# The low-part and the high-part products of split weights, in runs of eight blocks

## The chip, the cores and the metric

The kernel runs on one core of a Trainium2 chip. The metric is the time of one execution on the device, in microseconds. It is the median of three executions, and it is set beside one more execution that the hardware profiler recorded.

## The reference

The reference is a decoder trunk of two layers over one sequence of 256 tokens with 1024 channels, in float32. Cut to what matters here:

```
for i in (0, 1):
    hn = rmsnorm(h, norm_mix[i])
    mixed = short_conv_mixer(hn, ...) if i == 0 else dilated_attention_mixer(hn, ...)
    h = h + mixed
    h = h + square(relu(rmsnorm(h, norm_mlp[i]) @ mlp_w_up[i])) @ mlp_w_down[i]
    h = h + sigmoid(rmsnorm(h, norm_ple[i]) @ ple_w_gate[i]) * (p[i] @ ple_w_proj[i])
return rmsnorm(h, norm_final)
```

The short convolution needs three products of the width of h and one more; the attention has three groups of eight heads (a window of 128 with step 1, of 512 with step 4, of 2048 with step 16), so its query, key and value weights are 1024 x 9216. The MLP's weights are 1024 x 4096 and 4096 x 1024. Nearly all of the work is matrix products of weights by 256 columns of activations.

## The kernel before

**Products in two parts.** Every float32 weight and every activation is split in two: a high part rounded to the matmul's format (`whi`, made by ScalarE, L332) and the rest (`wlo`, made by VectorE, L333, through the helper `sub` at L281). A product is the sum of three matmuls: low weights by high activations, high weights by low activations, high weights by high activations. The weights come from memory in slabs of eight 128 x 128 blocks, in the order in which the plan first needs them; `split_to` splits them up to five slabs ahead of their use.

**The plan.** `make_plan` writes out one list of steps by hand. A step is a block (one 128 x 128 block of weights, by 256 columns of activations) or a `("do", ...)` step, which reads finished sums and makes the next activations. All engines work through instructions issued in this order; a scheduler may move those of the other engines, but the matmuls keep it.

**Kinds of blocks.** There are three:
- `"n"`: three matmuls of 256 columns, into one half of a PSUM bank.
- `"w"`: two matmuls. The activations' high and low parts lie next to each other (`x[2]`, 512 columns), so the high weights take both in one matmul of 512 columns, and the low weights take the high part in one of 256 columns. They go into a bank of their own, whose two halves `sums` adds later. There are 1296 of these blocks by the plan: 512 for the products `acc_u` of the two layers' MLP up, 384 for `acc_d` (down, all but the last quarter of each), 336 for `acc_qk` (queries and keys of heads 1 to 7) and 64 for `acc_X` (one third of the convolution's input product).
- `"t"`: the activations are the stationary operand and the weights move, 384 or 512 columns, three matmuls (`acc_v`, and `acc_g` and `acc_p` of the last stage).

The `"w"` blocks come in pairs, half 0 and half 1 (two neighbouring blocks of weights, the same activations). Half 0 is issued low then high, half 1 high then low, so that on TensorE two low products (256 columns each) and two high products (512 columns each) alternate.

Of the kernel before, what the change touches and what calls it, by code (L numbers as in the profile page):

```python
# [31 lines left out]
HURRY = 250  # L32
URGENT = ("gate_out", "mix_out", "down_out", "begin")
LOOK = 5
RAW_BUFS, SPLIT_BUFS, ACT_BUFS, PAIR_BUFS = 5, 6, 13, 20


# [168 lines left out]
def width(key):  # L206
    return {"v": GROUPS, "gate1": 4, "proj1": 4}.get(key, 1)
# [32 lines left out]
def tile_trunk(ctx: ExitStack, tc: tile.TileContext, plan, slabs, ap, out):  # L240
# [25 lines left out]
    def bank(name):  # L266
        return psum.tile([P, 2, S], F32, tag="ps", name=name)
# [9 lines left out]
    def flat(t):  # L277
        return t.rearrange("p i s -> p (i s)")
# [15 lines left out]
    acc, left, opened = {}, {}, set()  # L294
    for op in plan:
        if op[0] != "do":
            key = ((*op[4], op[5]), 0) if op[0] == "w" else (op[4], op[5] if op[0] == "n" else 0)
# [7 lines left out]
    offsets, n = [], 0  # L305
# [19 lines left out]
    def split_to(last):  # L325
        while len(parts) <= min(last, len(slabs) - 1):
            si = len(parts)
            load_to(si + RAW_BUFS - 1)
            t, width = loaded[si]
            hi = split_pool.tile([P, SLAB * P], F32R, tag="whi", name=f"whi{si}")  # L330
            lo = split_pool.tile([P, SLAB * P], F32R, tag="wlo", name=f"wlo{si}")
            nc.scalar.activation(hi[:, :width], t[:, :width], AF.Copy)  # L332
            sub(lo[:, :width], t[:, :width], hi[:, :width])  # L333
            parts.append((hi, lo))

    def weights(item):
        si, at = place[item]
        split_to(si + min(LOOK, 1 + si // 3))
        hi, lo = parts[si]
        n = width(item[0]) * P  # L340
        return hi[:, at : at + n], lo[:, at : at + n]

    def block(kind, key, k, col, name, half, operand, m=0, cuts=1):
        name = (*name, half) if kind == "w" else name
        if name not in opened:
            acc[name] = bank("acc_" + "_".join(map(str, name)))
        left[name, half if kind == "n" else 0] -= 1
        whi, wlo = weights((key, k, col))
        x = state[operand][k // 2]
        if kind == "n":  # L350
            dst = acc[name][:, half, :]
            products = ((dst, wlo, x[0][:, k % 2, :]), (dst, whi, x[1][:, k % 2, :]), (dst, whi, x[0][:, k % 2, :]))
        elif kind == "w":

            dst = acc[name]
            products = ((dst[:, 0, :], wlo, x[0][:, k % 2, :]), (flat(dst), whi, flat(x[2][:, k % 2, :, :])))

            products = products[::-1] if half else products
        else:
            n = width(key) * P // cuts  # L360
            whi, wlo = (t[:, m * n : (m + 1) * n] for t in (whi, wlo))
            dst = flat(acc[name])[:, :n]
            xhi, xlo = (t[:, k % 2, half * P : (half + 1) * P] for t in x[:2])
            products = ((dst, xhi, whi), (dst, xhi, wlo), (dst, xlo, whi))
        for n, (to, a, b) in enumerate(products):
            nc.tensor.matmul(  # L366
                to,
                a,
                b,
                start=n == 0 and name not in opened,  # L370
                stop=n == len(products) - 1 and left[name, half if kind == "n" else 0] == 0,
                skip_group_check=True,
            )
            opened.add(name)
# [391 lines left out]
        scores=scores, turn=turn, spread=spread, values=values,  # L766
        last_load=last_load, turn_h=turn_h, last_gate=last_gate, last_out=last_out, last_rms=last_rms, last_scale=last_scale,
    )
    for op in plan:
        if op[0] != "do":  # L770
            block(*op)
        elif op[1] in URGENT:
            with tc.high_priority(offset=HURRY):
                steps[op[1]](*op[2:])
        else:
            steps[op[1]](*op[2:])
# [87 lines left out]
```

## Time and profile before

| What | Value |
|---|---|
| median of three executions | 795.62 us (795.31 to 795.94) |
| the profiled execution, its own time | 797.34 us |
| its span, from the first to the last instruction | 795.5 us |
| TensorE (PE) busy | 776.2 us, 98% of the span |
| weight loads of TensorE (PEld) | 711.6 us, 89% |
| VectorE (DVE), ScalarE (ACT), GpSimd (POOL) busy | 582.1, 436.6, 177.2 us |
| mean granted clock of TensorE | 0.994 of full speed |

The profile tells for each instruction when it started and how long it took, and for each wait what ended it. A matmul's end is modelled and matmuls overlap, so a matmul's cost is read from the distance between the starts of neighbours, not from its own duration. The profiled execution's span and its own time are 1.8 us apart, and that time is 1.7 us above the median.

### The profile page before, as it was taken

What the parts mean: (1) busy time and instruction counts of PE and PEld (TensorE: products, weight loads), DVE (VectorE), ACT (ScalarE), POOL (GpSimd) and SP (SyncE); (2) the same over time, 40 slices, a digit from 0 to 9 for tenths busy, and PEclk for the clock granted to TensorE, in tenths of its full rate; (3) what the DMA queues carried; (4) which work ended last, traced back from release to release, by engine and by line L of the source; (5) the groups of instructions that cost most, each with busy time, mean ns of one, the idle gap of its engine ahead of it and who ended that gap; (6) DMA issues with size and microseconds to landing.
All of it is one profiled execution on the core that took longest, in us unless ns stands there. A gap on an engine that the chain in (4) does not pass through costs nothing.

```text
span 795.5 us, 12797 instructions
## 1 busy us (share of the span) xinstructions
PE 776.2 (98%) x4986; PEld 711.6 (89%) x4986; DVE 582.1 (73%) x818; ACT 436.6 (55%) x672; POOL 177.2 (22%) x117
## 2 busy tenths in 40 slices
PE   8999999999999999996999999999999999999996
PEld 7999998888888999986999999999988888888985
DVE  6987789898556669747678679679598887555555
ACT  7654565565444447527647546646475555444453
POOL 0000000000000000298587677678000000000001
PEclk9999999999999999998999999999999999999999
DMA  8866555656556555643464455456556655555521
GB/s 277 287 211 193 183 187 181 198 187 196 185 186 188 185 163 168 203 128 115 150 186 144 154 180 159 159 159 200 174 159 189 198 188 191 185 185 189 184 78 54
DMA packets 41676, 140.98 MB, mean 177 GB/s; under 512 B 4752, under 2 KB 5136, under 8 KB 41616
## 3 DMA queue, kind: packets, MB, share of 16 engines
q1 hardware_dynamic: 41616, 140.17, 55.7%
q8 instruction: 39, 0.64, 0.3%
q14 instruction: 21, 0.17, 0.1%
HBM read 139.10 MB, written 1.05 MB: 176 GB/s over the span
## 4 chain that ended last, share of the span: by engine, by line
PE 87%; DVE 5%; POOL 3%; ACT 2%; issue 2%; DMA 1%; SPq 0%; POOLq 0%; DVEq 0%; ACTq 0%
PE acc_d L366 23%; PE acc_u L366 22%; PE acc_qk L366 13%; PE acc_v L366 7%; PE acc_o L366 6%; PE acc_g L366 5%; PE acc_B L366 2%; PE acc_X L366 2%; DVE wlo L281 2%; PE acc_C L366 2%; POOL rot L612 2%; PE tp L662 1%; PE o L683 1%; PE sc L644 1%; ACT whi L332 1%
## 5 line engine op out<-in xcount | busy, mean ns | idle before, releaser
L281 DVE TENSOR_TENSOR wlo<-raw,whi 128x1024 fp32r<-128x1024 f32 (+3 forms) x273 | 364.5, 1343 | 130.0 <-ACT whi L332 127.9
L332 ACT ACTIVATE whi<-raw 128x1024 fp32r<-128x1024 f32 (+3 forms) x273 | 276.3, 1018 | 201.4 <-PE acc_d L366 82.0
L366 PE MATMUL acc_d<-u,whi 128*128 128x512 f32 (+1 forms) x640 | 166.8, 351 | 0.0
L366 PE MATMUL acc_u<-x,whi 128*128 128x512 f32 x512 | 161.0, 396 | 0.0
L366 PE MATMUL acc_qk<-x,whi 128*128 128x512 f32 (+1 forms) x432 | 122.9, 371 | 0.0
L438 POOL TENSOR_TENSOR n<-v,power 128x4 f32<-128x4 f32 (+1 forms) x6 | 6.5, 1085 | 512.2 <-DVE v L458 509.4
L366 PEld LDWEIGHTS acc_u<-x,wlo 128*128 128x128 f32 x512 | 96.4, 188 | 22.4
L366 PEld LDWEIGHTS acc_d<-u,wlo 128*128 128x128 f32 x512 | 96.9, 189 | 17.0
L366 PE MATMUL acc_d<-u,wlo 128*128 128x256 f32 x512 | 111.8, 279 | 0.0
L366 PE MATMUL acc_u<-x,wlo 128*128 128x256 f32 x512 | 101.3, 278 | 0.0
L366 PEld LDWEIGHTS acc_d<-u,whi 128*128 128x128 f32 x640 | 98.5, 190 | 0.0
L612 POOL TENSOR_TENSOR rot<-qk,sinr 16x512 f32<-16x512 f32 x48 | 87.0, 1813 | 3.3
L366 PEld LDWEIGHTS acc_qk<-x,wlo 128*128 128x128 f32 x384 | 72.4, 188 | 14.2
L366 PE MATMUL acc_qk<-x,wlo 128*128 128x256 f32 x384 | 82.5, 281 | 0.0
L366 PEld LDWEIGHTS acc_u<-x,whi 128*128 128x128 f32 x512 | 78.0, 189 | 0.1
L366 PE MATMUL acc_v<-whi,x 128*128 128x384 f32 x256 | 69.8, 343 | 0.0
L366 PEld LDWEIGHTS acc_qk<-x,whi 128*128 128x128 f32 x432 | 66.1, 189 | 0.0
L609 POOL TENSOR_TENSOR qk<-qk,cosr 128x512 f32<-128x512 f32 x24 | 37.9, 1578 | 57.9 <-DVE qk L386 44.6
L366 PEld LDWEIGHTS acc_v<-whi,x 128*128 128x128 f32 x256 | 47.4, 191 | 0.0
L366 PE MATMUL acc_o<-y,whi 128*128 128x256 f32 x256 | 46.0, 284 | 0.0
L366 PE MATMUL acc_v<-wlo,x 128*128 128x384 f32 x128 | 43.3, 339 | 0.0
L618 POOL TENSOR_TENSOR qk<-qk,rot 48x512 f32<-48x512 f32 x24 | 42.8, 1784 | 1.7
(164 smaller groups left out, 1029.6 us busy)
## 6 DMA issues: line engine op xcount, KB each, us to landing
raw<-in_w SPq DMA_DIRECT2D x232, 512.0 KB, 3.7
raw<-in_w SPq DMA_DIRECT2D x32, 384.0 KB, 3.1
raw<-in_w SPq DMA_DIRECT2D x7, 256.0 KB, 5.7
h<-in_xT SPq DMA_DIRECT2D x4, 256.0 KB, 6.0
out<-ht SPq DMA_DIRECT2D x4, 256.0 KB, 2.0
pt<-in_pT SPq DMA_DIRECT2D x2, 256.0 KB, 4.6
mask<-in_mask SPq DMA_DIRECT2D x2, 256.0 KB, 4.3
gain<-in_gain SPq DMA_DIRECT2D x2, 256.0 KB, 4.2
```

The source lines that it names most:

```text
L281: nc.vector.tensor_tensor(out, a, f32(b), ALU.subtract)
L332: nc.scalar.activation(hi[:, :width], t[:, :width], AF.Copy)
L366: nc.tensor.matmul(to, a, b, start=n == 0 and name not in opened, stop=n == len(products) - 1 and left[name, half if kind == "n" else 0] == 0,
L438: nc.gpsimd.tensor_tensor(y, v, power[:, : v.shape[1]], ALU.pow)
L609: nc.gpsimd.tensor_tensor(t, p, both(cosr), ALU.mult)
L612: nc.gpsimd.tensor_tensor(r[dst : dst + 16], p[src : src + 16], sinr[src : src + 16].unsqueeze(1).to_broadcast([16, 2, S]), ALU.mult,)
L618: nc.gpsimd.tensor_tensor(t[:48], t[:48], r[:48], ALU.add)
L644: nc.tensor.matmul(ps[:, (g + 1) * P : (g + 2) * P], t[:, 0, own], t[:, 1, own], start=True, stop=True)
L662: nc.tensor.transpose(ps[n // 2][:, n % 2, b * P : (b + 1) * P], sm[:, n * P : (n + 1) * P], ident)
L683: nc.tensor.matmul(ps[:, 0, b * P : (b + 1) * P], v12[:, b, g * P : (g + 1) * P], t[:, g, b * P : (b + 1) * P], start=False, stop=g == 1, ...
```

## The change

The new function `blocks` takes a run of `"w"` blocks and issues first all their low products, then all their high ones. The loop over the plan collects `"w"` blocks until eight are together or the next step is not one. The other kinds are issued as before. The number, the shapes and the operands of the matmuls stay the same; what changes is their order, which matmul opens and which ends the sum of a bank, and with it when a bank is ready to be read.

```
+RUN = 8
...
+    def blocks(ops):
+
+        for part in (0, 1):
+            for op in ops:
+                block(*op, part=part)
+
-    def block(kind, key, k, col, name, half, operand, m=0, cuts=1):
+    def block(kind, key, k, col, name, half, operand, m=0, cuts=1, part=None):
...
-        left[name, half if kind == "n" else 0] -= 1
+        left[name, half if kind == "n" else 0] -= part != 0
...
-            products = ((dst[:, 0, :], wlo, x[0][:, k % 2, :]), (flat(dst), whi, flat(x[2][:, k % 2, :, :])))
-
-            products = products[::-1] if half else products
+            products = ((dst[:, 0, :], wlo, x[0][:, k % 2, :]), (flat(dst), whi, flat(x[2][:, k % 2, :, :])))[part:][:1]
...
-                stop=n == len(products) - 1 and left[name, half if kind == "n" else 0] == 0,
+                stop=part != 0 and n == len(products) - 1 and left[name, half if kind == "n" else 0] == 0,
...
-    for op in plan:
-        if op[0] != "do":
+    run = []
+    for op, behind in zip(plan, [*plan[1:], ("do",)]):
+        if op[0] == "w":
+            run.append(op)
+            if behind[0] != "w" or len(run) == RUN:
+                blocks(run)
+                run = []
+        elif op[0] != "do":
             block(*op)
```

How the instructions stand now is seen at two places. The first is TensorE in the MLP up of layer 0, third pair of column blocks (`acc_u_2_0` and `acc_u_2_1` are the banks of half 0 and half 1, `x1_0` and `x1_1` two pairs of activation tiles, `whi43` and `wlo43` the parts of one slab). Before, eight matmuls in a row:

```order
L366 MATMUL acc_u_2_0_1494<-x1_0_1205,wlo43_1343 128x256
L366 MATMUL acc_u_2_0_1494<-x1_0_1205,whi43_1342 128x512
L366 MATMUL acc_u_2_1_1503<-x1_0_1205,whi43_1342 128x512
L366 MATMUL acc_u_2_1_1503<-x1_0_1205,wlo43_1343 128x256
L366 MATMUL acc_u_2_0_1494<-x1_0_1205,wlo43_1343 128x256
L366 MATMUL acc_u_2_0_1494<-x1_0_1205,whi43_1342 128x512
L366 MATMUL acc_u_2_1_1503<-x1_0_1205,whi43_1342 128x512
L366 MATMUL acc_u_2_1_1503<-x1_0_1205,wlo43_1343 128x256
```

And now, in the same place, the last four low products of a run and its first four high ones:

```order
L371 MATMUL acc_u_2_0_1494<-x1_1_1227,wlo43_1343 128x256
L371 MATMUL acc_u_2_1_1502<-x1_1_1227,wlo43_1343 128x256
L371 MATMUL acc_u_2_0_1494<-x1_1_1227,wlo43_1343 128x256
L371 MATMUL acc_u_2_1_1502<-x1_1_1227,wlo43_1343 128x256
L371 MATMUL acc_u_2_0_1494<-x1_0_1205,whi43_1342 128x512
L371 MATMUL acc_u_2_1_1502<-x1_0_1205,whi43_1342 128x512
L371 MATMUL acc_u_2_0_1494<-x1_0_1205,whi43_1342 128x512
L371 MATMUL acc_u_2_1_1502<-x1_0_1205,whi43_1342 128x512
```

Equal widths now follow each other eight at a time, and neighbouring matmuls always write to different banks. A run of eight here uses one slab, as its eight blocks did before.

The second place is VectorE where the softmax of head 0 is made (`sm0_0`, `sm0_1` the scores of the two halves of the tokens, `st...` their row statistics, `qk_1_2` the sums of head 1's third group, `wlo132` a slab to be split). Before:

```order
L386 TENSOR_TENSOR qk_1_2_3964<-acc_qk_1_2_0_3888,qk_1_2_3964 128x256
L647 ISA sm0_0_3940,st0_0_0_3941<-sc0_0_3934,mask0_3461 128x512
L647 ISA st0_0_0_3941 128x1
L386 TENSOR_TENSOR qk_1_2_3964<-acc_qk_1_2_1_3897,qk_1_2_3964 128x256
L650 TENSOR_SCALAR st1_0_0_3942<-st0_0_0_3941 128x1
L647 ISA sm0_1_3955,st0_0_1_3956<-sc0_1_3949,mask1_3463 128x512
L647 ISA st0_0_1_3956 128x1
L281 TENSOR_TENSOR wlo132_3977<-raw132_3834,whi132_3976 128x1024
L650 TENSOR_SCALAR st1_0_1_3957<-st0_0_1_3956 128x1
```

And now:

```order
L391 TENSOR_TENSOR qk_1_2_3964<-acc_qk_1_2_0_3888,qk_1_2_3964 128x256
L391 TENSOR_TENSOR qk_1_2_3964<-acc_qk_1_2_1_3896,qk_1_2_3964 128x256
L652 ISA sm0_0_3940,st0_0_0_3941<-sc0_0_3934,mask0_3461 128x512
L652 ISA st0_0_0_3941 128x1
L282 TENSOR_TENSOR wlo132_3977<-raw132_3834,whi132_3976 128x1024
L655 TENSOR_SCALAR st1_0_0_3942<-st0_0_0_3941 128x1
L652 ISA sm0_1_3955,st0_0_1_3956<-sc0_1_3949,mask1_3463 128x512
L652 ISA st0_0_1_3956 128x1
L655 TENSOR_SCALAR st1_0_1_3957<-st0_0_1_3956 128x1
```

The second sum of `qk_1_2` and the split of slab 132 moved ahead; the nine instructions up to the second negated maximum (the last row) are the same ones.

## Rows read from the trace of the kernel before

**Rows 1.** The page, busy us of each engine, share of the span, instructions.
```profile
PE 776.2 (98%) x4986; PEld 711.6 (89%) x4986; DVE 582.1 (73%) x818; ACT 436.6 (55%) x672; POOL 177.2 (22%) x117
```

**Rows 2.** Waits of TensorE, first two of five: us in total, times, longest.
```profile
PE tp L662 <- ACT sm L653: 7.0, 1, 7.0
PE acc_p L366 <- DVE wlo L281: 2.2, 3, 1.4
```

**Rows 3.** Chain that ended last: start us, us, what, number of matmuls.
```profile
38.62 5.58 PE acc_X L366 x32
...
84.14 23.04 PE acc_o L366 x192
...
129.71 66.89 PE acc_u L366 x384
196.60 89.92 PE acc_d L366 x576
...
394.75 6.24 PE acc_v L366 x36
...
777.33 2.04 PE acc_g L366 x9
```

**Rows 4.** A stretch of MLP up: busy us of each engine, granted clock.
```profile
core 0: us, PE busy (x) PEld busy (x) DVE busy (x) ACT busy (x) POOL busy (x), PEclk, DMA share, GB/s
129.71:196.60 66.89, 66.89 (x386) 58.44 (x386) 58.72 (x89) 40.06 (x64) 0.00 (x0) 1.00 0.61 189
```

**Rows 5.** Order of time, PE, MLP up: start us, us, instructions merged.
```profile
139.90 0.39 PE L366 MATMUL acc_u<-x,wlo 128*128 128x256 f32 x2
140.13 0.63 PE L366 MATMUL acc_u<-x,whi 128*128 128x512 f32 x2
140.59 0.40 PE L366 MATMUL acc_u<-x,wlo 128*128 128x256 f32 x2
```

**Rows 6.** Order of time, PE, where 512 columns follow a run of 256.
```profile
757.86 0.40 PE L366 MATMUL acc_g<-whi,x 128*128 128x512 f32 x1
...
759.02 0.62 PE L366 MATMUL acc_g<-whi,x 128*128 128x512 f32 x2
...
760.15 0.39 PE L366 MATMUL acc_g<-wlo,x 128*128 128x512 f32 x1
```

**Rows 7.** Order of time, PE, 512 columns a little behind transposes.
```profile
764.00 0.40 PE L366 MATMUL acc_g<-wlo,x 128*128 128x512 f32 x1
...
766.31 0.39 PE L366 MATMUL acc_g<-whi,x 128*128 128x512 f32 x1
```

**Rows 8.** Order of time, PE, where 256 columns follow a run of 512.
```profile
785.78 0.39 PE L366 MATMUL acc_g<-whi,x 128*128 128x512 f32 x1
786.01 0.28 PE L366 MATMUL acc_p<-whi,p 128*128 128x256 f32 x1
786.12 0.28 PE L366 MATMUL acc_p<-wlo,p 128*128 128x256 f32 x1
786.24 0.40 PE L366 MATMUL acc_p<-whi,p 128*128 128x256 f32 x2
786.48 0.28 PE L366 MATMUL acc_p<-wlo,p 128*128 128x256 f32 x1
```

**Rows 9.** Weight loads of two groups: busy us, mean ns of one, idle before.
```profile
L366 PEld LDWEIGHTS acc_u<-x,wlo 128*128 128x128 f32 x512 | 96.4, 188 | 22.4
L366 PEld LDWEIGHTS acc_u<-x,whi 128*128 128x128 f32 x512 | 78.0, 189 | 0.1
```

**Rows 10.** Order of time, VectorE, before the stall at head 0.
```profile
363.93 0.68 DVE L647 CUSTOM_DVE_ANT_0 sm<-sc,mask 128x512 f32<-128x512 f32 x1
...
364.53 0.42 DVE L386 TENSOR_TENSOR qk<-acc_qk,qk 128x256 f32<-128x256 f32 x1
...
365.53 1.69 DVE L281 TENSOR_TENSOR wlo<-raw,whi 128x1024 fp32r<-128x1024 f32 x1
367.15 0.14 DVE L650 TENSOR_SCALAR st<-st 128x1 f32<-128x1 f32 x1
```

**Rows 11.** Order of time, ScalarE, the last exponential before the stall ends.
```profile
367.33 0.72 ACT L651 ACTIVATE sm<-sm,st 128x512 f32<-128x512 f32 x1 [1.29 <-DVE st L650]
```

## The prediction

> **What bounds the kernel now.** I read the page's busy times first: TensorE is busy for 98% of the span [rows 1]. The second view is TensorE's waits: the longest is one stall of 7.0 us before the transposes of head 0, and the next, 2.2 us, lies at the start [rows 2]. So the time is a queue of matmuls on one engine, and an edit that keeps their number counts only by what it does to the distance between the starts of neighbours. The third view is the chain of waits in order of time, because its long pieces give that distance as a mean over hundreds [rows 3]. The reader is to see four numbers there:
> - 256 columns behind 256 columns: 23.04 us / 192 = 120.0 ns each (`acc_o`).
> - One `"w"` block in today's order: 66.89 us / 192 blocks = 348.4 ns (`acc_u`, 384 matmuls); `acc_X` gives 5.58 / 16 = 348.8. `acc_d` is the sum of both: 192 blocks at 348.4 ns and 192 matmuls at 120 ns make 89.9 us, and 89.92 stand there.
> - 384 columns behind 384: 6.24 / 36 = 173.3 ns (`acc_v`).
> - 512 columns behind 512: 2.04 / 9 = 226.7 ns (`acc_g`).
>
> From 256 to 384 and from 384 to 512 columns each step adds 53.3 ns, so in a stretch of one width a matmul costs 13.3 ns plus its columns at 0.417 ns. By that, a block would cost 120.0 + 226.7 = 346.7 ns, and it costs 348.4. The fourth view, TensorE's instructions in order of time, shows how: two low products take 0.23 us from start to start and two high ones 0.46 us [rows 5], that is 115 and 232 ns each. In the mixture the 512s cost some 6 ns more than in a stretch of their own, and the 256s some 5 ns less. The difference of the sums, 1.7 ns a block, is what the order costs today.
>
> **The change part by part.** Nothing is added or removed: the 1296 `"w"` blocks keep their two matmuls. By the order of the changed program they stand in 161 runs of eight and two of four, as much as 162 runs of eight, and every run uses one slab. So there are 162 places where 512s follow 256s, and not 648.
>
> *Eight low products.* In a stretch of their own they cost 8 x 120.0 = 960 ns. The first ones behind 512s are cheaper: at the end of the program four matmuls of 256 columns behind 512s take 786.48 - 786.01 = 0.47 us [rows 8], where four at 120 take 0.48. So 10 ns are given back, as the two low products give back today (0.23 for 0.24). I take 950 ns.
>
> *Eight high products.* In steady state 8 x 226.7 = 1813 ns. No row shows more than two 512s of this kind in a row; the nearest are the 512s of the last stage, where the activations are stationary and the weights move. There the first 512s behind 256s are dear: the five from 757.86 to 759.02 take 232 ns each, the five from there to 760.15 take 226 [rows 6]. That is 5 x 232 - 5 x 226.7 = 27 ns for the transition, after which the steady cost is reached. In the stretch from 764.00 to 766.31 ten of them take 2.31 us [rows 7], 44 ns over ten steady ones, so 35 ns for eight. At the other end, if only the first two paid, as many as stand together today (0.46 us for 0.453), it would be some 10 ns. I take 27 ns, because that stretch follows 256-column matmuls as the runs will.
>
> *The run.* 950 + 1813 + 27 = 2790 ns, against 8 x 348.4 = 2787 ns today: +3 ns a run, or 162 x 3 = **+0.5 us**. With 10 ns for the transition it is 2773, -14 a run, -2.3 us; with 35 it is 2798, +11 a run, +1.8 us. The main case is thus no change within about 2 us: the few transitions that remain cost more each, because more 512s stand behind them to pay.
>
> *When things are needed.* A run begins with its low products, as a pair did, so `wlo` of a slab is needed at the same moment; `whi` is needed 8 x 120 = 0.96 us later instead of 0.12. No split is due earlier, and raw tiles and split buffers turn over with the slab as before. In MLP up TensorE is busy for the whole 66.89 us while VectorE has 8 us and ScalarE 27 us free [rows 4]; that cover hides the splits, and without it each slab would show up to VectorE's split, 1.69 us [rows 10]. Where an MLP begins, the low parts of the activations are needed 0.84 us later. No wait of this kind is in [rows 2], so I count nothing.
>
> *When sums are ready.* Half 0's last product now ends one 512 before half 1's, 0.23 us, and not 0.35. Its two reading steps start 0.12 us later, on engines for which TensorE does not wait in these stages. The banks opened for half 1 are taken 0.12 us earlier; nothing in [rows 2] waits for a bank. I count nothing.
>
> *The stall at head 0.* TensorE waits there for ScalarE's scaled exponentials, which follow the second exponential at 367.33 [rows 11], and that follows VectorE's second negated maximum at 367.15 [rows 10]. VectorE's order ahead of it changes: the sum (0.42 us) and the split (1.69 us) each move ahead of a score step (0.68 us), but the same instructions stand before the negated maximum. So it comes at the same time; the first exponential comes later and can push the second by at most its own overlap, some 0.3 us. I take 0 and keep 0.3 for the range.
>
> The sum is +0.5 us. It is made against the profiled execution's span of 795.5 us (797.34 as its own time, 1.7 above the median). Applied to the median of the runs shown, 795.62, it gives 796.1 us.
>
> **The rivals.**
> - *The 512s stay at 233 ns, the 256s go to 120: slower.* The place is inside the run of high products. Here the price of a 512 would hang on what it is (weights stationary, both activation parts moving) and not on its neighbours; two of them together cost 0.46 us today [rows 5]. The low products lose the cheap position behind 512s. A run is then 8 x (120 + 232.5) = 2820 ns, +33 ns, +5.3 us, 800.9 us. It decides if the fourth to eighth 512 of a run still cost over 230 ns. Against it: 256s cost 120 whether weights or activations move in them [rows 3, 8], and the 13.3 ns hold at three widths, so the moving operand does not set the price. Chance 0.15.
>
>   [...]
> - *Only transitions cost: faster.* If the 1.7 ns a block were the price of today's 648 transitions and a longer run paid no more at each, 162 of them would keep a quarter, and 3/4 x 1.7 x 1296 = 1.7 us are saved: 793.9 us. For it: the 512s do settle at 226.7. Against it: [rows 6] and [rows 7] show five to ten dear ones at a transition, not two. Chance 0.28.
> - *Both the cheap rates hold: much faster.* Low products at 115 and high at 226.7 would give 162 x 8 x (348.4 - 341.7) = 8.7 us, 786.9 us. Against it: every long stretch of 256s runs at 120. Chance 0.04.
> - *A wait elsewhere appears*, from the new order on VectorE and ScalarE: about 1 to 3 us slower. Chance 0.05.
>
> **How the numbers follow.** The main case has 0.48, by itself from 794.4 to 797.7: a transition of 17 ns makes a run 2780 ns, -7 ns, -1.2 us; one of 35 ns gives +1.8 us, and the stall 0.3 more. Cheaper transitions are the second rival. A measurement of this kernel can tell about 0.2%, 1.6 us, from no change. Of the main case 0.08 lies above that and 0.40 within. Of the second rival, whose time lies on the bound of 794.0, 0.17 lies below and 0.11 within. The first rival and three fifths of the last are slower; the third is faster. Faster: 0.17 + 0.04 = 0.21; slower: 0.08 + 0.15 + 0.03 = 0.26; within: 0.40 + 0.11 + 0.02 = 0.53. The range goes from 793.5, where a transition costs 10 ns or a little more, to 800.9, the first rival.
>
> **What would show it.** In order of time, in MLP up: low products of a run start 115 to 120 ns apart and mostly 120; the first four or five high ones 230 to 236, the last ones 226 to 227; the chain's piece of 384 matmuls takes 66.8 to 67.1 us. If all eight high ones stay at 232, the first rival is right, and the piece takes 67.7 us. If the high ones fall to 227 from the third on, it takes 66.5. The stall at head 0 stays at 7 us. What would make the prediction wrong besides is a cost that today's order never shows, such as a dearer switch from the low to the high products of one slab.

## The result and the profile after

The changed kernel takes 798.3 us (median of eight runs, 797.68 to 799.01), the kernel before 795.95 us (median of eight, 795.19 to 796.28). The ratio is 1.0029 [1.002, 1.0038], so the change costs 2.3 us (1.6 to 3.0). The forecast was 796.1 us, with a range from 793.5 to 800.9; the time lies inside the range, but above the 0.2% within which the main case was to lie. The differences in us here and below are those of the ratio, with its interval; they can lie up to 0.7 us from the difference of the two medians.

The profiled execution of the changed kernel has a span of 795.9 us and 797.68 us as its own time, the lowest of the eight; the profiled one of before has 795.5 and 797.34, above all eight of before. So the two spans, 0.4 us apart, say little, and the pieces have to be compared one by one. One piece that differs and has nothing to do with the change is the start: this piece of `acc_X` starts at 36.85 us, where it started at 38.62 [rows 3]. The waits for the first split weights, 2.2 us before, are missing in this trace. The second experiment below has the order of before up to there, and its piece starts at 36.85 us too.

The first view is the page's busy times of the kernel after, us, share of the span and instructions:

```profile
PE 777.0 (98%) x4986; PEld 715.6 (90%) x4986; DVE 583.0 (73%) x818; ACT 439.0 (55%) x672; POOL 179.1 (23%) x117
```

TensorE is busy for 0.8 us more than in [rows 1], with the same 4986 matmuls. The second view is TensorE's waits of the kernel after (us in total, times, longest):

```profile
PE tp L667 <- ACT sm L658: 8.7, 1, 8.7
PE warm L510 <- DVE power L506: 1.0, 1, 1.0
```

The stall at head 0 was to stay at 7.0 us [rows 2] and takes 8.7. The wait of 2.2 us at the start is gone; that is the start told of above. The third view is the chain of the kernel after (start us, us, what, number of matmuls):

```profile
36.85 5.59 PE acc_X L371 x32
...
82.41 23.04 PE acc_o L371 x192
...
128.05 67.04 PE acc_u L371 x384
195.09 90.07 PE acc_d L371 x576
...
601.25 67.05 PE acc_u L371 x384
```

The piece of MLP up takes 67.04 and 67.05 us in the two layers, against 66.89 [rows 3]: 349.2 ns a block, not 348.4. The granted clock is 1.00 in it, as it was [rows 4]. `acc_o`, which holds no blocks of the changed kind, has not moved. The fourth view is TensorE's instructions in order of time in that piece:

```profile
140.02 2.00 PE L371 MATMUL acc_u<-x,whi 128*128 128x512 f32 x8
141.86 1.11 PE L371 MATMUL acc_u<-x,wlo 128*128 128x256 f32 x8
142.81 2.00 PE L371 MATMUL acc_u<-x,whi 128*128 128x512 f32 x8
144.65 1.12 PE L371 MATMUL acc_u<-x,wlo 128*128 128x256 f32 x8
```

From start to start, eight high products take 1.84 us (140.02 to 141.86) and eight low ones 0.95 (141.86 to 142.81). Averaged by their place in the run, over the 135 runs of eight that follow a 512 and are followed by a 256, the distance from each start to the next is, in ns:

```
place in the run      1      2      3      4      5      6      7      8     sum
low products        113.4  119.2  120.0  120.0  120.0  120.0  120.0  120.0   952.5
high products       233.3  235.9  228.3  232.5  230.8  226.7  226.7  226.8  1841.0
```

A run is 2793.5 ns, the forecast was 2790, and before it was 2787. So the mechanism is the forecast one: five dear 512s, then the steady 226.7. The size is 6.3 ns a run instead of 3, and 162 x 6.3 = 1.0 us instead of 0.5.

The fifth view is VectorE in order of time before the stall ends, in the kernel after (start us, us, instruction and how many are merged in the row; what it waited for in brackets):

```profile
358.89 0.70 DVE L282 TENSOR_TENSOR qk<-qk,qk 128x512 fp32r<-128x512 f32 x1 [8.48 <-ACT qk L410]
359.50 0.75 DVE L391 TENSOR_TENSOR qk<-acc_qk,qk 128x256 f32<-128x256 f32 x2
360.18 3.17 DVE L282 TENSOR_TENSOR wlo<-raw,whi 128x768 fp32r<-128x768 f32 x2
363.27 0.74 DVE L391 TENSOR_TENSOR qk<-acc_qk,qk 128x256 f32<-128x256 f32 x2
363.93 0.67 DVE L652 CUSTOM_DVE_ANT_0 sm<-sc,mask 128x512 f32<-128x512 f32 x1
...
364.54 2.32 DVE L282 TENSOR_TENSOR wlo<-raw,whi 128x1024 fp32r<-128x1024 f32 x1
...
366.85 0.68 DVE L652 CUSTOM_DVE_ANT_0 sm<-sc,mask 128x512 f32<-128x512 f32 x1
...
367.56 0.15 DVE L655 TENSOR_SCALAR st<-st 128x1 f32<-128x1 f32 x1
```

The same stretch of before, of which [rows 10] showed the end:

```profile
360.23 0.69 DVE L281 TENSOR_TENSOR qk<-qk,qk 128x512 fp32r<-128x512 f32 x1 [8.47 <-ACT qk L405]
360.84 0.42 DVE L386 TENSOR_TENSOR qk<-acc_qk,qk 128x256 f32<-128x256 f32 x1
361.23 0.96 DVE L281 TENSOR_TENSOR wlo<-raw,whi 128x768 fp32r<-128x768 f32 x1
362.11 0.42 DVE L386 TENSOR_TENSOR qk<-acc_qk,qk 128x256 f32<-128x256 f32 x1
362.45 1.23 DVE L281 TENSOR_TENSOR wlo<-raw,whi 128x1024 fp32r<-128x1024 f32 x1
```

From the split of head 1's first group to the second negated maximum it was 360.23 to 367.15, 6.92 us [rows 10]; now it is 358.89 to 367.56, 8.67 us: 1.75 us more, as much as the stall grew. The instructions are the same, and two of them are longer. The splits of the two slabs behind the first sums took 0.96 and 1.23 us, and now 0.96 and 2.23, merged into 3.17 above; the split behind the first score step took 1.69 and now 2.32. Together that is 5.49 us (3.17 + 2.32) where it was 3.88, 1.61 more. In MLP up, where GpSimd is idle [rows 4], all 24 splits of 128x1024 in the trace of before took 1.21 to 1.23 us.

What lies beside them is on GpSimd. Its rows in order of time, before:

```profile
362.67 2.13 POOL L609 TENSOR_TENSOR qk<-qk,cosr 128x512 f32<-128x512 f32 x1 [3.14 <-DVE qk L386]
364.88 3.47 POOL L612 TENSOR_TENSOR rot<-qk,sinr 16x512 f32<-16x512 f32 x2
```

And after:

```profile
360.33 1.93 POOL L614 TENSOR_TENSOR qk<-qk,cosr 128x512 f32<-128x512 f32 x1 [2.13 <-DVE qk L391]
362.34 3.44 POOL L617 TENSOR_TENSOR rot<-qk,sinr 16x512 f32<-16x512 f32 x2
365.85 2.13 POOL L623 TENSOR_TENSOR qk<-qk,rot 48x512 f32<-48x512 f32 x1
367.95 1.26 POOL L614 TENSOR_TENSOR qk<-qk,cosr 128x512 f32<-128x512 f32 x1
```

GpSimd's rotary step of head 1's second group (a product with the cosine, two with the sine, an addition) waits for both sums of `qk_1_1`. With the products in runs the second sum follows the first at once, ahead of the split of 768 columns, where it stood behind it. So the rotary step starts 1.4 us after the split of `qk` (360.33 - 358.89), and not 2.4 us (362.67 - 360.23).

The rows fit a strict taking of turns between a split and a product on GpSimd, whole instructions at a time, the one that begins first going at its own speed. GpSimd's product with the cosine takes 1.26 us where no split stands beside it, as at 367.95 in the kernel after. VectorE's sums, with one operand in PSUM, took no longer beside a product: the two at 363.27 in the kernel after take 0.74 us together inside a product with the sine, and the two at 359.50, beside none, 0.75. Follow the ends:

- Before, the split of 1024 columns at 362.45 is first and takes 1.23 us, to 363.68; the product that begins at 362.67 ends at 364.80, 1.12 us behind that. Only the split at 365.53 [rows 10] comes second, in the middle of the first product with the sine (364.88 to 366.14), and takes 1.69.
- After, the split at 360.18 is first, the product with the cosine ends at 362.26 behind it, and the second split ends at 363.35, 1.1 us behind the product: it came second. The third split begins at 364.54, and ends at 366.86, 1.1 us behind the end of the products with the sine at 365.78: second again, by nearly a whole product. GpSimd's addition, which begins at 365.85, ends 1.1 us behind the split, at 367.98.

So two splits wait out most of a product each, where one waited for part of one: the split that began first took 1.23 us, those that began second 2.23 and 2.32. The turns are the author's reading of these rows; why the two engines hold each other up is not shown.

This stall also has a price behind it. TensorE's granted clock is 0.50 from 366.18 to 373.00 us before and from 365.66 to 372.49 after, and 1.00 ahead of that and behind. It fell while TensorE was idle in the stall (from 361.84 us before and from 360.51 after) and rose while it worked again. The transposes that end the stall start at 368.81 and 369.23, so 4.2 us of work ran at the low clock before and 3.3 after. That gave 0.42 us back to this trace of the kernel after: the blocks behind start at 373.78 in both. In the second experiment below the low clock lasts until 374.25, over 5.5 us of work. So the same stall does not cost the same in each trace.

### The profile page after: what moved, and what is told of

The parts are those of the page before. It is cut to its first block, busy times and chain, and to the rows that moved or that the text cites. A ratio compares the mean times of both kernels' runs of the same rounds, so it can differ in the third digit from the quotient of the medians.

```text
span 795.9 us, 12768 instructions
## 1 busy us (share of the span) xinstructions
PE 777.0 (98%) x4986; PEld 715.6 (90%) x4986; DVE 583.0 (73%) x818; ACT 439.0 (55%) x672; POOL 179.1 (23%) x117
## 4 chain that ended last, share of the span: by engine, by line
PE 89%; POOL 3%; DVE 3%; ACT 2%; issue 1%; DMA 0%; SPq 0%; POOLq 0%; DVEq 0%; ACTq 0%
PE acc_d L371 23%; PE acc_u L371 22%; PE acc_qk L371 13%; PE acc_v L371 7%; PE acc_o L371 6%; PE acc_g L371 5%; PE acc_B L371 3%; PE acc_X L371 3%; PE acc_C L371 3%; POOL rot L617 2%; DVE wlo L282 1%; PE tp L667 1%; PE o L688 1%; PE sc L649 1%; POOL qk L623 1%
## 5 line engine op out<-in xcount | busy, mean ns | idle before, releaser
L371 PE MATMUL acc_d<-u,whi 128*128 128x512 f32 (+1 forms) x640 | 142.2, 349 | 0.0
L371 PE MATMUL acc_u<-x,whi 128*128 128x512 f32 x512 | 128.2, 392 | 0.0
L371 PEld LDWEIGHTS acc_u<-x,whi 128*128 128x128 f32 x512 | 92.1, 189 | 16.5
L371 PE MATMUL acc_qk<-x,whi 128*128 128x512 f32 (+1 forms) x432 | 101.5, 368 | 0.0
L371 PE MATMUL acc_d<-u,wlo 128*128 128x256 f32 x512 | 89.8, 282 | 0.0
L371 PEld LDWEIGHTS acc_d<-u,wlo 128*128 128x128 f32 x512 | 76.9, 191 | 3.8
L371 PEld LDWEIGHTS acc_u<-x,wlo 128*128 128x128 f32 x512 | 69.6, 190 | 4.7
L371 PE MATMUL acc_u<-x,wlo 128*128 128x256 f32 x512 | 71.4, 282 | 0.0
L371 PE MATMUL acc_qk<-x,wlo 128*128 128x256 f32 x384 | 61.0, 284 | 0.0
L371 PEld LDWEIGHTS acc_qk<-x,wlo 128*128 128x128 f32 x384 | 54.3, 190 | 2.3
```

The lines of the kernel that those rows point to most:

```text
L371: nc.tensor.matmul(to, a, b, start=n == 0 and name not in opened, stop=part != 0 and n == len(products) - 1 and left[name, half if kind == ...
```

## The experiments

All were timed beside the kernel before: the two on head 1's blocks and the runs of 16 and of 1 on one chip (before: 796.22 us), the other four on another (before: 796.06 us). None leaves out any of the computation.

**Head 1's q and k blocks in pairs, all else in runs.** If the stall grows because of the order on VectorE, then giving back the old order to the `"w"` blocks of head 1 alone takes the stall back to 7.0 us and leaves the price of the runs.

```
     products = (...)
+    products = products[part:][:1] if part is not None else products[::-1] if half else products
...
-        if op[0] == "w":
+        if op[0] == "w" and op[4][:2] == ("qk", 1):
+            block(*op)
+        elif op[0] == "w":
             run.append(op)
```

> The change as it is, except that the query and key blocks of head 1 (48 of the 1296) keep the order of before. My theory: the changed kernel lost its time in two places, a run of eight costs 2793 ns and not 2787 (about 1.0 us over 156 runs), and the stall at head 0 is 1.7 us longer because both sums of head 1's second group now go ahead of a weight split on VectorE, which sets GpSimd's rotary steps off about 1 us earlier and beside VectorE's splits. Then here the stall is back at 7.0 us (6.9 to 7.2) and the kernel is 0.6 to 1.1 us slower than before. Rival: the stall grew because TensorE's and GpSimd's work came at another time for any reason, or it varies from run to run; then it stays at 8.5 us or more and the kernel 2 us or more slower.

Measured: 797.04 us, ratio 1.0007 [0.9998, 1.0015], +0.6 us (-0.2 to +1.2). First the longest wait of TensorE in this kernel, then, from its chain, the piece of MLP up:

```profile
PE tp L668 <- ACT sm L659: 7.0, 1, 7.0
```

```profile
128.51 67.04 PE acc_u L372 x384
```

The stall is back at 7.0 and the piece is still 67.04. By the traces the greater part of the loss is the stall, 1.7 us against some 1.0 for the runs.

**The kernel before, with head 1's q and k blocks alone in runs.** The counterpart: the condition is turned round (`!= ("qk", 1)` goes to `block`), so only 48 of the 1296 blocks change.

> The kernel before, with head 1's query and key blocks alone in runs of eight (6 runs). My theory: the stall at head 0 grows to 8.7 us (8.4 to 9.0) and the kernel is 1.5 to 1.9 us slower than before, since the runs' own cost is absorbed in the stall. Rival (the loss of the changed kernel lies in the runs of eight themselves, over all stages): within 0.3 us of before.

Measured: 797.96 us, ratio 1.0018 [1.001, 1.0027], +1.4 us (0.8 to 2.1). Longest wait, and piece of MLP up:

```profile
PE tp L668 <- ACT sm L659: 8.7, 1, 8.7
```

```profile
127.94 66.89 PE acc_u L372 x384
```

The same 8.7 us with MLP up as before. The two parts, 0.6 and 1.4 us, add up to 2.0 of the 2.3 us of the whole change.

**Runs of 16, of 4 and of 1.** To settle what a run costs, head 1 in pairs as in the first experiment and only the length changed:

```
-RUN = 8
+RUN = 16
```

> As the first of these, with runs of sixteen where the plan has sixteen such blocks in a row (73 runs of sixteen, the others of eight). My theory: each change from 256 to 512 columns and back costs 20 ns over the steady 120.0 and 226.7, however long the run; 73 of them go, 1.5 us less than with runs of eight, so 0.3 to 0.8 us faster than before, and the chain's piece of 384 matmuls in MLP up takes 66.8 us. Rival (the dear 512s come again later in a long run, or the low parts of two slabs are not ready): 67.0 us or more, and no faster than with runs of eight.

Measured: 795.65 us, ratio 0.9989 [0.9981, 0.9998], -0.9 us (-1.5 to -0.2). From the chain, MLP up, and then TensorE in order of time inside it:

```profile
128.31 66.81 PE acc_u L372 x384
```

```profile
139.28 2.08 PE L372 MATMUL acc_u<-x,wlo 128*128 128x256 f32 x16
141.20 3.82 PE L372 MATMUL acc_u<-x,whi 128*128 128x512 f32 x16
144.85 1.36 PE L372 MATMUL acc_u<-x,wlo 128*128 128x256 f32 x10
```

Sixteen low products take 1.92 us from start to start and sixteen high ones 3.65. On the mean of 52 runs behind 512s it is 1912.5 and 3654.5 ns, 7.5 ns under sixteen at 120.0 and 27 to 28 over sixteen at 226.7. The transition is the same as in a run of eight and is paid half as often. (The trace has 77 runs of sixteen, not 73.)

With `RUN = 4`:

> The changed kernel with runs of four (head 1 in the order of before). Theory (after a change of width the first five 512s are dear, by 233, 236, 228, 232 and 231 ns, then 226.7; the first two 256s give back 7 ns): four low products cost 473 and four high ones 930 ns, 350.6 ns a block, the piece of 384 matmuls 67.3 us, the kernel 2.2 to 3.2 us slower than before. Rival (a cost that falls steadily with the number of changes of width, so that runs of four lie between runs of two, 348.4, and of eight, 349.2): 348.8 ns, 67.0 us, 0.3 to 0.9 us slower.

Measured: 798.85 us, ratio 1.0036 [1.0024, 1.0049], +2.9 us (1.9 to 3.9), with the stall at 7.0. MLP up, from the chain:

```profile
128.44 67.36 PE acc_u L372 x384
```

That is 350.8 ns a block, and the theory was right. A run of four is dearer than one of eight and than the pairs of before: on the mean of 286 runs its four high products cost 929 ns, 22 more than four at 226.7, and nearly all of a transition's price falls on four blocks.

With `RUN = 1` low and high products alternate:

> As the first of these, with runs of one: every block low then high, 256 and 512 columns in turn. Theory A (a 512 behind 256s is dear by 6.6 ns and the 256 behind it gives back most): 233 + 114.5 = 347 to 348 ns a block, the piece of 384 matmuls at 66.7 us, 0.5 to 1.5 us faster than before. Theory B (each change of width costs the 1.8 ns that today's order shows on average): 350.4 ns a block, 67.3 us, 2.5 us slower.

Measured: 799.75 us (796.47 to 801.06), ratio 1.0036 [1.0024, 1.0048], +2.9 us (1.9 to 3.8); the profiled run is the fastest, 796.47. MLP up in layer 0 and in layer 1, from its chain:

```profile
128.96 67.84 PE acc_u L372 x384
...
601.00 66.56 PE acc_u L372 x384
```

Both theories miss: theory A's 347 to 348 ns come near one layer only, and theory B's 350.4 ns stand in neither, though its 2.5 us lie in the interval. The same 384 matmuls in the same order take 353.3 ns a block in one layer and 346.7 in the other, in one execution, and the second is the steady sum 120.0 + 226.7 with nothing on top. TensorE in order of time shows that it is a beat kept up through each stretch. Layer 0, then layer 1:

```profile
139.87 0.40 PE L372 MATMUL acc_u<-x,whi 128*128 128x512 f32 x1
140.11 0.28 PE L372 MATMUL acc_u<-x,wlo 128*128 128x256 f32 x1
140.23 0.40 PE L372 MATMUL acc_u<-x,whi 128*128 128x512 f32 x1
...
620.02 0.39 PE L372 MATMUL acc_u<-x,whi 128*128 128x512 f32 x1
620.25 0.28 PE L372 MATMUL acc_u<-x,wlo 128*128 128x256 f32 x1
620.37 0.39 PE L372 MATMUL acc_u<-x,whi 128*128 128x512 f32 x1
```

From start to start the 512s take 241, 236 and 233 ns in turn in layer 0, and 230 each in layer 1; the 256s take 116.7 on the mean in both. The granted clock is 1.00 in both, and the 256s take the same, so it isn't that. All stretches of layer 0 in this trace (`acc_X`, `acc_u`, `acc_d`) have the dear beat, those of layer 1 the cheap one; what sets the beat is open. If the number of stretches in each beat changed from run to run, that would explain why this kernel's times spread over 4.6 us. This is not shown, since only the one execution has a trace.

**The rotary step of head 1's second group held back.** On the changed kernel, to test whether it is GpSimd beside the splits, and not the mere order on VectorE, that lengthens the stretch. A one-column copy by VectorE, placed behind the scores, is made an input of that rotary step.

```
-        return [("do", "add_up", ("qk", h, g)), ("do", "qk_out", h, g)]
+        steps = [("do", "add_up", ("qk", h, g)), ("do", "qk_out", h, g)]
+        return steps[:1] if (h, g) == (1, 1) else steps
...
+    def late_rotary():
+        nc.vector.tensor_copy(cur["qk", 1, 1][1][:, 0, 0:1], last_stat[0])
...
-    plan += ... + steps[late ^ 1] + sums(h, 2)
+    plan += ... + steps[late ^ 1] + ([("do", "late_rotary"), ("do", "qk_out", 1, 1)] if late else []) + sums(h, 2)
```

> The changed kernel, with GpSimd's rotary step of head 1's second group held back behind the softmax of head 0: VectorE copies one column into that step's output tile behind the second negated maximum, and the step stands there in the plan. VectorE's order before that point stays that of the changed kernel. Theory (the stall grew because VectorE's splits ran beside GpSimd's steps): the splits of slabs 130, 131 and 132 take 0.96, 1.23 and 1.23 us again and not 3.17 and 2.32 together, the stall shrinks from 8.7 to 6.5 to 7.0 us, and the kernel is 0.4 to 1.2 us slower than before. Rival (the order on VectorE itself makes the stall longer, by what stands ahead of the second maximum): the stall stays at 8.4 us or more, the kernel 2 us or more slower.

Measured: 797.8 us, ratio 1.0023 [1.0013, 1.0033], +1.8 us (1.0 to 2.6); the stall is 7.6 us, a miss of both. The views are TensorE's longest wait, VectorE's splits and GpSimd's rows, both in order of time:

```profile
PE tp L675 <- ACT sm L665: 7.6, 1, 7.6
```

```profile
360.93 3.16 DVE L283 TENSOR_TENSOR wlo<-raw,whi 128x768 fp32r<-128x768 f32 x2
...
365.29 1.22 DVE L283 TENSOR_TENSOR wlo<-raw,whi 128x1024 fp32r<-128x1024 f32 x1
```

```profile
361.15 4.06 POOL L619 TENSOR_TENSOR rot<-qk,sinr 16x512 f32<-16x512 f32 x2 [2.20 <-DVE qk L393]
365.29 2.33 POOL L616 TENSOR_TENSOR qk<-qk,cosr 128x512 f32<-128x512 f32 x1
```

The edit held back half of what it meant to. The copy writes a column that the product with the cosine overwrites, so that product moved behind the third group's rotary step; the two products with the sine, which only read the sums, went ahead, and lie beside the first two splits, which take 3.16 us as in the changed kernel. But the third split now begins just as those products have ended (365.22), is first, and takes 1.22 us instead of 2.32: 1.1 us less, which is what the stall lost (8.7 to 7.6). The product with the cosine that begins at the same moment, the third group's, is the one that waits: 2.33 us instead of 1.26. So with one order on VectorE the same split is dear when it comes second and cheap when it comes first, and order alone, the rival, doesn't explain it. By the ratios the loss is some 0.5 us smaller than the changed kernel's, less than the intervals can tell.

**The kernel before, with the split of head 1's first group moved behind the transposes.** That split waits 8.5 us for ScalarE on VectorE (its row above), with the softmax's first steps queued behind it. Moved behind head 0's transposes, it no longer holds them.

```
-        if g == 0:
+        if g == 0 and head != 1:
             split_into("qk", head, t)
...
-        plan += v(h, range(6)) + steps[2 - late] + v(h, range(6, NK)) + ...
+        plan += v(h, range(6)) + steps[2 - late] + ([("do", "qk_split")] if late else []) + v(h, range(6, NK)) + ...
```

> The kernel before, with the split of head 1's first query-key group (one step on ScalarE and one on VectorE, needed only by the scores of head 1) moved behind the transposes of head 0. Theory: the stall at head 0 exists because that split waits for GpSimd for 8.5 us at the head of VectorE's queue and 12 us at the head of ScalarE's, with the softmax behind it; then the stall falls from 7.0 us to 0 to 1.5 us, and the kernel is 5 to 7 us faster than before. Rival (GpSimd's chain of rotary steps is the bound, and the wait comes back at the scores of head 1): a wait of 3 us or more there, 0 to 3 us faster.

Measured: 794.3 us, ratio 0.998 [0.9971, 0.9989], -1.6 us (-2.3 to -0.9). The stall before the transposes is gone, and another has come. TensorE's longest wait, TensorE at its end, and what GpSimd does just ahead of it:

```profile
PE sc L651 <- POOL qk L618: 5.4, 2, 4.6
```

```profile
378.28 0.80 PE L651 MATMUL sc<-qk 128*128 128x128 f32 x2 [4.65 <-POOL qk L618]
```

```profile
372.23 4.06 POOL L612 TENSOR_TENSOR rot<-qk,sinr 16x512 f32<-16x512 f32 x2
376.37 1.86 POOL L618 TENSOR_TENSOR qk<-qk,rot 48x512 f32<-48x512 f32 x1
```

The rival was right: behind the 7.0 us lies GpSimd's chain of rotary steps, on which head 1's scores wait for 4.6 us, and head 0's, earlier, for the other 0.7 of the 5.4. So 7.0 - 5.4 = 1.6 us are to be had, and 1.6 came. The low clock stays, now behind the new wait: 0.50 from 376.00 to 382.83 us.

**Runs of 16 everywhere, with that split moved.** The two edits that gained, together; head 1's blocks are in runs as well.

> Runs of sixteen everywhere, head 1 too, and that split moved in the same way. If the two effects add up: as the version before this one and 0.3 to 0.9 us faster still, 5.5 to 7.5 us faster than before. If runs in head 1 still set GpSimd off too early, the stall is 1 to 2 us longer than in the version before this one.

Measured: 793.56 us, ratio 0.9969 [0.9959, 0.998], 2.5 us faster than before (1.6 to 3.3), and faster than both kernels. Its longest wait and its MLP up:

```profile
PE sc L657 <- POOL qk L624: 5.4, 2, 4.7
```

```profile
127.98 66.81 PE acc_u L372 x384
```

The expectation missed the size for the same reason as the last, GpSimd's chain. Runs in head 1 do not make this wait longer (4.7 against 4.6 us). The gains add, within the intervals: 1.6 from the stall and 0.9 from the runs of 16, as each gave alone.

## Why the prediction was right and wrong

- **What bounds the kernel**: right. What the change did is all on TensorE's queue and in its one long stall. What it did not count is the low clock behind that stall (4.2 us of work before, 3.3 after).
- **Eight low products, 950 ns**: 952.5. They give back 7.5 ns, nearly all in the first of them, and not 10. Right but for 2.5 ns, less than the 0.01 us to which the rows told it.
- **Eight high products and the transition, 1813 + 27 ns**: 1841.0. The five dear ones and the fall to 226.7 are as the first 512s of the last stage showed them; their excess is 27.7 ns. The rows that were chosen for it were the right ones.
- **The run, "+3 ns a run, or 162 x 3 = +0.5 us"**: the mechanism held, the term was undersized: +6.3 ns, +1.0 us. The first experiment, which holds this term alone, measured +0.6 (-0.2 to +1.2), and the pieces of 67.04 us (forecast 67.0 for 2790 ns) stand for it.
- **When things are needed, when sums are ready, counted at nothing**: right in the MLPs, where no new wait appeared. But the sums' times were looked at only for the engines that TensorE waits for there. That "its two reading steps" move closer together in head 1 is what set GpSimd off earlier.
- **"The stall at head 0 ... I take 0 and keep 0.3"**: this is the step that failed. It argued that "the same instructions stand before the negated maximum. So it comes at the same time". The instructions are the same, but not their durations: two of the three splits came to begin with nearly a whole product on GpSimd ahead of them, where one had begun in the middle of one, and the three took 5.49 us instead of 3.88. That is most of the 1.75 us by which the stall grew. Of the 1.61 us, 1.00 lies in a split ahead of the nine instructions that were compared beforehand: there the second sum of `qk_1_1` had moved ahead of a split, too. The second experiment shows that head 1's order brings it, with MLP up unchanged, and the held-back rotary step shows that a split is short again (1.22 us) where GpSimd has just ended. [rows 10] had the hint: one split of 1.69 us, which the prediction took for the split's price, where the same shape had taken 1.23 us three microseconds earlier and in all of MLP up.
- **Sum**: 1.0 + 1.75 = 2.8 us by the traces, against 2.3 (1.6 to 3.0) measured; 0.42 us came back in the profiled execution by the shorter low clock. That the time of 798.3 lies inside the range is luck in part. By itself the main case ended at 797.7, 2.1 us above the time it started from. The range reached further up only for the first rival, which did not happen; the longer stall took the time there.
- **The rivals.** *The 512s stay at 233*: out, the last three of a run cost 226.7. *Only transitions cost*: its premise, that a longer run pays no more at each, is out at runs of eight. Per change from low to high and back, over the steady 346.7 ns a block, the pieces of MLP up (66.89, 67.36, 67.04 and 66.81 us for 192 blocks) give 3 ns for a run of two (before), 17 for four, 20 for eight and 21 for sixteen. It grows until the five dear ones are inside the run, and changes by no more than a nanosecond from there, so the gain that this rival had in mind comes with sixteen. *Both the cheap rates*: out, the low products of a run cost 119 ns on the mean, not 115. *A wait elsewhere, from the new order on VectorE*, with "about 1 to 3 us" and a chance of 0.05: this is what happened besides the main case, though the wait was an old one that grew, and its chance was far too low.

## What to carry to other kernels

The length of a run of equal matmuls has a price: here two, four, eight and sixteen blocks in a row cost 348.4, 350.8, 349.2 and 348.0 ns each. At eight and at sixteen it is a price of 20 and 21 ns for each change of width and back, which the longer run spreads over more blocks; runs of two pay only 3 ns. Why the first five 512s of a run are dear is not shown. Where a change of order leaves "the same instructions" before a wait, look up what other engines do beside them: here a split of 128x1024 took 1.23 us where it began first and up to 2.32 where it began second. Such a duration belongs to its neighbours too, and two durations of one shape in one stretch (1.23 and 1.69 us before) were the sign of it. And before a stall is worked on, find the wait that lies under it; here 7.0 us were in sight and 1.6 to be had. Look at the granted clock behind it as well: here the work after the stall ran at half of it for 3.3 to 5.5 us.

## What was not expected of the hardware

- Strictly alternating 256s and 512s run in one of two beats, 353.3 or 346.7 ns for a pair, in the same execution and with the same instructions; what selects the beat is open.
- Behind 256s the 512s aren't evenly dear: 233, 236, 228, 232 and 231 ns, then 226.7 to the end of the run.
- The rows of VectorE's subtraction of two operands in SBUF and of GpSimd's products fit a taking of turns, a whole instruction at a time: in the rows above 128x1024 on VectorE took 1.22 to 1.23 us where it began first, and up to 2.32 where it began second; a product of 128x512 on GpSimd 1.26 us alone, and up to 2.33 where it began second.
- The low clock behind the stall (0.50) covered 4.2, 3.3 and 5.5 us of TensorE's work in three traces with stalls of 7.0, 8.7 and 8.7 us.
